# Outputs return on a list of their own; spatial weights and eight token blocks are turned by VectorE

## The chip, the core and the metric

The kernel runs on one core of one Trainium2 chip. TensorE (PE) multiplies, VectorE (DVE) and ScalarE (ACT) work element by element, GpSimd (POOL) and SyncE (SP) mostly issue DMAs, and 16 DMA engines move data between DRAM and the core's SBUF. [...] The metric is the device time of one execution in microseconds, the median of several runs; less is better.

## The reference, cut to what matters

One step of a decoder trunk with one layer, for a prompt of 256 tokens and 8 sample rows of one token, with a model width of 2048. A conditioning projection gives six vectors `sh, sc, gt` per row. Then:

```python
h = rmsnorm(x, g_pre_mix) * (1 + sc1) + sh1
z = h @ w_in                                   # splits into three branches and their gates
v = layernorm(gelu(z_v)); y_a = gelu(z_u) * (tril(w_s) @ v + b_s)      # 8 groups of 128x128
o, S = gated_linear_recurrence(q, k, v, log_f, s0)                     # y_b: HGRN2, 8 heads; y_c: GLA, 4 heads
merged = sum(sigmoid(z_gate[n]) * (y[n] @ w_branch[n]) for n in range(3))
x = x + gt1 * rmsnorm(merged @ w_out, g_post_mix)
h2 = rmsnorm(x, g_pre_mlp) * (1 + sc2) + sh2
x = x + gt2 * rmsnorm(square(relu(h2 @ w_mlp_up)) @ w_mlp_down, g_post_mlp)
```

Outputs are x for the prompt and the samples, the final recurrent states of both, and the normalised `v` rows of the samples. All is float32.

## The kernel before, in words

**Products.** Activations lie with channels on partitions and tokens (256 + 8 = 264, `NT`) along the free axis. A weight tile of 128x128 is the stationary operand and 264 tokens move. Each float32 product is made of three in a faster form: weights and activations are split into a high and a low part (`whi`, `wlo`), ScalarE makes the high part (L673), VectorE the low one (L677). `linear` makes a block of 256 output channels from granules of 1024 weight columns by 128 rows each; splits run two granules ahead (`SPLIT_AHEAD`), loads five (`LOAD_AHEAD`), weights come on SP's queue. A block accumulates in one of two PSUM buffers (`pmm`), which the next block but one needs back.

**Buffers.** 28 blocks of 128x1056 float32 (`NBLK`, `blk()`) hold activations and many temporaries.

**Stages.** First the conditioning and the first part of `w_in`, over k in five chunks (`CHUNKS`); in the last of these the loop counts `gi` from 0 to 19. Then the GLA inputs, branch 0 with spatial gating (`mixer_a`), the gates of branch b (`gate_tiles(5120)`), branch 1 (HGRN2, groups 0 and 1), the gates of branch c, branch 2 (GLA, group 2), the output projection (8 blocks `m`), the norms between, and the MLP in 8 slices with up and down projections; the last slice of the down projection ends the kernel.

**Order.** TensorE's and POOL's order is that of the program in the mixer stages; in the output projection and the MLP TensorE's alone is. VectorE and ScalarE are put in order by the compiler's scheduler in these stages, in order of program where it sees no wait. Each engine runs its own list strictly in order. Work of the mixers is written as generators on lists: `bg` (mixers, one after the other), `bs` (sample rows), `bt` (turns through DRAM). `background()` is called after each granule, one slot: it adds a rate to what a list may spend (`RATES` 1.8 to 1.0 for `bg`, 0.5 for `bs`, `TURN_RATE` 0.35 for `bt`) and steps the list's first generator; a step costs what it yields (1 for a bare `yield`). A generator that yields a function holds its whole list until it is true; `READY` holds it to the next slot. What is queued in `later` runs at the next slot. `finish(i)` drains the list up to group i's mixer before its outputs are used.

**Two ways to turn.** A 128x128 block is turned by TensorE against the identity into PSUM (L96; `to_tokens` does four of them for one block of two channel tiles by 256 tokens). Or through DRAM with the class `Rows`: `half` turns 32x32 squares with VectorE (L850), `out` writes 512 KB to `rows_d` (L853), `back` reads it in four DMAs of 128 KB that place the squares (L859); a copy then puts the rows in natural order. `TURN_OUT` and `TURN_IN` ask for two slots between these.

**What the change touches.** In `mixer_a` the spatial weights are turned by 8 TensorE transposes and masked with `triu` out of PSUM. In `mixer_r` the key block `kd` and the head outputs go through `Rows`; the mixer waits for both on its list (`kd_rows.come`, copies at L1462; `out.come`, `out.there`, copies at L1492), and only then does the list go on to the next mixer's `gates` (L1175 to L1179). Branch 1 begins with `parts_b`, that is `finish(0)`, `finish(1)` and the splits of `yparts` (L145, L148); its gate values leave PSUM by a `Tanh` at L1543. In the output projection each block is scaled (`gated`), turned by `to_tokens` one slot later, multiplied with the residual rows and squared for sums (`products` L1646, `squares` L1650), and copied to rows `og` (`put_rows` L1653, L1654). In the last slice of the down projection the same goes to `yt` without sums. `PRE_AT` names the blocks of the output projection at which two loads each (four blocks) of the sixth conditioning round are issued (L379).

Of the kernel before, what the change touches and what calls it, by code (L numbers as in the profile page):

```python
# [15 lines left out]
P = 128  # L16
# [30 lines left out]
N_PRE = 6  # L47
PRE_AT = (2, 3, 4)
ADA_BATCH = (4, 8)
# [23 lines left out]
def hybrid_step_kernel(  # L73
# [759 lines left out]

    rows_d = dp.tile([13, P, 1024], F32, tag="rows_d", name="rows_d")
    n_turned = [0]
# [69 lines left out]
    def const_a(src):  # L905
        consts_a.append(blk([P, 8, P]))
        nc.sync.dma_start(consts_a[-1], src)

    srcs_a = [
        sgu_ln_g[0].partition_broadcast(P).rearrange("p (g n) -> p g n", g=8),  # L910
        sgu_ln_b[0].partition_broadcast(P).rearrange("p (g n) -> p g n", g=8),
        sgu_w_s[0].rearrange("g n m -> n g m"),
        sgu_b_s[0].rearrange("g n -> (g n)").partition_broadcast(P).rearrange("p (g n) -> p g n", g=8),
# [34 lines left out]
    def mixer_a():  # L948
        lng, lnb, wsr, bsb = consts_a
        lng, lnb = (v.rearrange("p g n -> p (g n)") for v in (lng, lnb))  # L950
# [3 lines left out]
        for gg in range(2):  # L954
            ps = sm()
            for i in range(4):
                T.transpose(ps[:, i * P:(i + 1) * P], wsr[:, 4 * gg + i, :], ident)
            yield
            mul(wsT[:, 4 * gg:4 * gg + 4, :], ps.rearrange("p (g n) -> p g n", g=4), triu.unsqueeze(1).to_broadcast([P, 4, P]))
        yield  # L960
# [142 lines left out]
    for ci, n in enumerate(CHUNKS):  # L1103
# [5 lines left out]
        for gi in range(ng):  # L1109
# [35 lines left out]
            if final:  # L1145
                if gi in (6, 12, 18):
                    rounds.steps()
                if gi in (0, 2, 6, 8, 12, 14, 18):
                    rounds.load()
                if gi in (6, 7, 8, 9):  # L1150
                    rows_a.half((gi - 6) // 2, gi % 2)
                if gi in (8, 10):
                    rows_a.out(gi // 2 - 4)
                if gi in (11, 13):
                    rows_a.back((gi - 11) // 2)
                now[0] += 1
                if gi >= 12:
                    bg.pump(1.0)
# [163 lines left out]
    def mixer_r(G):  # L1322
# [98 lines left out]
        mul(kd, kd, k[:, :, 0:NP])  # L1421
        yield READY
        yield READY
        kd_rows = Rows([kd])
        yield from kd_rows.gone()
        attx = blk([P, 4, P])
        ps = sm([P, 4, P])
# [4 lines left out]
        del kd  # L1432
        yield from kd_rows.come()

# [7 lines left out]

        for hf in range(2):
            for h0 in range(0, 4, nh):
                ps = sm([P, nh, dv])
# [27 lines left out]
        for h0 in range(0, 4, nh):  # L1473
            so = blk([P, nh, dv])
            p0, p1 = sm([P, nh, dv]), sm([P, nh, dv])
            for i in range(nh):
                T.matmul(p0[:, i, :], kt[:, 0, (h0 + i) * P:(h0 + i + 1) * P], vr(0, h0 + i), start=True, stop=True)
                T.matmul(p1[:, i, :], kt[:, 1, (h0 + i) * P:(h0 + i + 1) * P], vr(1, h0 + i), start=True, stop=True)
            yield
            for i in range(nh):  # L1480
                S.activation(so[:, i, :], p0[:, i, :], AF.Copy, scale=ft[:, h0 + i:h0 + i + 1])
            add(so, so, p1)
            nc.gpsimd.dma_start(G.p_out(h0, nh), so)
            yield
        yield from out.come()
        yield out.there
        o = [blk() for _ in range(nj)]
        for a, rows in enumerate(out.rows):
            for hf in range(2):
                put = S.copy if hf else V.tensor_copy  # L1490
                for j in range(nj):
# [3 lines left out]
                    )  # L1495
                yield 0.6
        G.o = o

    def finish(i):
        bg.drain(gens[i])  # L1500
        G = Gs[i]
        while not hasattr(G, "os"):
            bs.drain(bs.g[0])
# [140 lines left out]
    def products(m, t, g, pt):  # L1644

        V.scalar_tensor_tensor(g[:, 1, 0:CW].rearrange("p (m f) -> p m f", m=2), in_rows(x1, t, m), 1.0, pt[:, t], ALU.mult, ALU.mult,  # L1646
                               accum_out=sums[:, 0, t, m:m + 1])

    def squares(m, t, g, pt):
        S.activation(g[:, 0, 0:CW].rearrange("p (m f) -> p m f", m=2), pt[:, t], AF.Square, accum_out=sums[:, 1, t, m:m + 1])  # L1650

# [4 lines left out]
    def block_rows(m, g):  # L1656
# [5 lines left out]
        for t in range(2):  # L1662
            squares(m, t, g, pt)

    def norms(meanwhile):
# [14 lines left out]

    sums = tmp([P, 2, 2, NS], "fs")
    pre = Rounds()
    pre.todo = [(5, k) for k in range(KT)]
    for m in range(8):
# [5 lines left out]
        if m < 7:  # L1690
            g = gated(m, z, G1)
            later.append((now[0], lambda m=m, g=g: block_rows(m, g)))
        if m == 6:

            S.activation(tmp([P, 1], "srr", 1), sqacc[:, 0:1], AF.Sqrt)
    rounds.drain()
    rounds = pre
# [36 lines left out]
    V.reduce_sum(both[:, :, 2:2 + NS], ps.rearrange("p s k b -> p s b k"), axis=mybir.AxisListType.X)  # L1734
    V.reduce_sum(both[:, :, 0:2], sums, axis=mybir.AxisListType.X)
    rounds.steps(3)
# [113 lines left out]
    def down(f, ah, al):  # L1850
        for m in range(8):
# [8 lines left out]
            if f == NFB - 1:  # L1860
                g = gated(m, dst, G2)
                later.append((now[0], lambda m=m, g=g: put_rows(m, to_tokens(g), yt)))

# [5 lines left out]
    for f in range(NFB):  # L1869
        nxt = up(f + 1) if f + 1 < NFB else None  # L1870
        if f == NFB - 1:
            rounds.drain()
            mul(G2, mod[:, 5 * KT:6 * KT, :], gpost2T.unsqueeze(2).to_broadcast([P, KT, NC]))
            yt = [[blk([P, 1024]) for _ in range(2)] for _ in range(2)]
        last = pend
        down(f, *pend)
# [151 lines left out]
```

## Time and profile before

| | |
|---|---|
| median of 3 runs | 1784.72 us (1784.36 to 1785.2) |
| profiled execution | 1786.63 us |
| its span, first to last instruction | 1784.6 us |
| mean granted TensorE clock | 0.998 |
| PEld, TensorE's weight loads, busy | 1676.9 us |
| DMA | 455.67 MB, mean 255 GB/s |

The page gives busy time by engine, then a row of 40 slices of the span. "Granted clock" is the share of full speed that TensorE had. The windows view gives, for a stretch in us from the start of the span: its length, the busy time of PE, PEld, DVE, ACT and POOL (with counts), the granted clock, the mean busy share of the DMA engines, and GB/s. The timeline gives start, length, engine, line, operation, and in brackets the engine's idle time before it and what ended that. In the lists of groups stand, after a bar, busy us, mean ns of one, and idle us before them with what ended it.

### The profile page before, as it was taken

The numbers are of one execution on the slowest core, as the hardware profiler recorded it, in microseconds if no ns is written. First come the engines' busy times: TensorE is split into PE (matmuls) and PEld (weight loads), VectorE is DVE, ScalarE is ACT, GpSimd is POOL, SyncE is SP. The second block draws the span as 40 slices with busy tenths as digits, with TensorE's granted clock in tenths as the row PEclk, the third lists the DMA queues.
The fourth block names the chain that finished last, engine by engine and source line by source line (L and its number), as shares of the span: only waits on it lengthen the run. The fifth ranks groups of instructions, "written<-read, shape, count | busy, mean of one in ns | idle before, by whom it ended". The sixth has DMA issues, their size and how long they took to land.

```text
span 1784.6 us, 42046 instructions
## 1 busy us (share of the span) xinstructions
PE 1760.2 (99%) x16866; PEld 1676.9 (94%) x16866; DVE 1194.0 (67%) x2096; ACT 999.7 (56%) x1810; POOL 175.6 (10%) x293
## 2 busy tenths in 40 slices
PE   6999999999999999999999999999999999999998
PEld 5899999999989989899999989999999999999997
DVE  5676669886687687666566666545666666666666
ACT  5444456667766665655555666545454545454554
POOL 4222010122111112220000010000000000000000
PEclk9999999999999999999999999999999999999999
DMA  9998699899999889998766847786666666666663
GB/s 345 395 354 297 224 327 306 253 331 325 301 290 311 284 276 333 347 374 281 222 193 217 310 124 238 234 263 197 193 198 193 198 194 196 195 196 196 195 195 115
DMA packets 334547, 455.67 MB, mean 255 GB/s; under 512 B 15986, under 2 KB 277984, under 8 KB 334352
## 3 DMA queue, kind: packets, MB, share of 16 engines
q1 hardware_dynamic: 312160, 381.05, 66.0%
q0 software_dynamic: 21552, 71.48, 11.6%
q8 instruction: 132, 2.16, 0.5%
q14 instruction: 63, 0.52, 0.1%
q10 hardware_dynamic: 640, 0.47, 0.1%
HBM read 434.42 MB, written 18.51 MB: 254 GB/s over the span
## 4 chain that ended last, share of the span: by engine, by line
PE 91%; DMA 4%; DVE 1%; issue 1%; ACT 1%; POOL 1%; SPq 0%; DVEq 0%; ACTq 0%; POOLq 0%
PE mm L92 83%; PE ada L92 4%; PE sm L92 3%; DMA raw<-in_w_in_dram 1%; DMA b<-in_w_ada_dram 1%; PE sm L96 1%; DVE wlo L677 0%; DMA b<-in_x_prompt_dram 0%; DMA out_dram<-st 0%; ACT whi L673 0%; DMA vbc<-vs_d 0%; POOL b L537 0%; DVE b L142 0%; DVE b L1768 0%; ACT b L148 0%
## 5 line engine op out<-in xcount | busy, mean ns | idle before, releaser
L92 PE MATMUL mm<-b,whi 128*128 128x264 f32 x9248 | 1580.1, 278 | 4.0 <-ACT gt L1543 2.9
L92 PEld LDWEIGHTS mm<-b,whi 128*128 128x128 f32 x9248 | 1397.2, 190 | 38.3 <-issue 19.8
L92 PE MATMUL mm<-b,wlo 128*128 128x264 f32 x4624 | 1278.8, 277 | 0.5 <-DVE wlo L677 0.5
L677 DVE TENSOR_TENSOR wlo<-raw,whi 128x512 fp32r<-128x512 f32 x1118 | 758.6, 689 | 421.9 <-ACT whi L673 419.1
L673 ACT CAST whi<-raw 128x512 fp32r<-128x512 f32 x1118 | 681.9, 617 | 635.0 <-DVE wlo L677 318.7
L92 PEld LDWEIGHTS mm<-b,wlo 128*128 128x128 f32 x4624 | 875.7, 189 | 1.1 <-DVE wlo L677 0.9
L142 DVE TENSOR_TENSOR b<-b,mm 128x528 f32<-128x528 f32 (+1 forms) x137 | 95.7, 699 | 71.7 <-PE mm L92 65.5
L1958 POOL TENSOR_TENSOR gs<-b,G 128x16 f32<-128x16 f32 x1 | 0.2, 222 | 713.9 <-DVE b L142 713.9
L92 PE MATMUL ada<-b,cT 128*32 128x256 f32 (+2 forms) x880 | 64.8, 419 | 2.8 <-DMA b<-in_w_ada_dram 2.8
L92 PEld LDWEIGHTS ada<-b,cT 128*32 128x32 f32 x880 | 25.9, 112 | 31.9 <-issue 16.2
L537 POOL DMA_DIRECT2D b<-in_w_ada_dram x64 | 46.3, 726 | 45.3 <-PE ada L92 36.0
L1307 POOL DMA_DIRECT2D out_dram<-st x32 | 23.5, 736 | 226.7 <-DVE st L1306 210.9
L673 ACT CAST whi<-araw 128x512 fp32r<-128x512 f32 x38 | 23.2, 618 | 28.4 <-PE mm L92 26.2
L92 PE MATMUL ada<-araw,cT 128*32 128x512 f32 x272 | 36.7, 599 | 0.0
L139 DVE TENSOR_TENSOR b<-b,b 128x512 f32<-128x512 f32 (+1 forms) x49 | 34.5, 721 | 2.2 <-ACT b L1367 0.7
L1304 ACT ACTIVATE st<-st,fs 128x128 f32<-128x128 f32 (+1 forms) x96 | 35.1, 427 | 0.0
L1306 DVE SCALAR_TENSOR_TENSOR st<-vbc,b,st 128x128 f32<-128x128 f32 (+1 forms) x96 | 32.2, 391 | 1.0 <-DMA vbc<-vs_d 1.0
L859 POOL DMA_DIRECT2D b<-rows_d x52 | 28.6, 556 | 31.1 <-DMA rows_d<-b 8.0
L677 DVE TENSOR_TENSOR wlo<-araw,whi 128x512 fp32r<-128x512 f32 x38 | 24.7, 686 | 1.7 <-ACT whi L673 1.6
L145 DVE TENSOR_TENSOR b<-b 128x1024 f32<-128x1024 f32 (+1 forms) x24 | 24.4, 1020 | 1.2 <-PE ada L92 1.1
L145 DVE TENSOR_TENSOR b<-gt,b 128x528 fp32r<-128x528 f32 x32 | 22.7, 711 | 3.2
L1842 ACT ACTIVATE b<-vt 128x528 fp32r<-128x528 f32 x32 | 22.8, 713 | 1.0
(307 smaller groups left out, 827.1 us busy)
## 6 DMA issues: line engine op xcount, KB each, us to landing
raw<-in_w_in_dram SPq DMA_DIRECT2D x225, 512.0 KB, 6.0
raw<-in_w_mlp_down_dram SPq DMA_DIRECT2D x128, 512.0 KB, 3.6
raw<-in_w_mlp_up_dram SPq DMA_DIRECT2D x125, 512.0 KB, 3.9
araw<-in_w_ada_dram SPq DMA_DIRECT2D x68, 512.0 KB, 6.8
b<-in_w_ada_dram SPq DMA_DIRECT2D x60, 512.0 KB, 6.7
b<-in_w_ada_dram POOLq DMA_DIRECT2D x48, 512.0 KB, 9.5
raw<-in_w_branch_dram SPq DMA_DIRECT2D x48, 512.0 KB, 4.9
raw<-in_w_out_dram SPq DMA_DIRECT2D x32, 512.0 KB, 4.6
```

The lines of the kernel that those rows point to most:

```text
L92: return nc.tensor.matmul(out, w, x, **kw)
L139: V.tensor_tensor(o, a, b, op=ALU.mult)
L142: V.tensor_tensor(o, a, b, op=ALU.add)
L145: V.tensor_tensor(o, a, b, op=ALU.subtract)
L537: queue.dma_start(w[:, i], w1[k * P:(k + 1) * P, :, self.k0 * P:(self.k0 + self.n) * P])
L673: self.last = [S.copy(hi, raw).ins, None]
L677: self.last[1] = V.tensor_tensor(lo, raw, hi.bitcast(F32), op=ALU.subtract).ins
L859: nc.gpsimd.dma_start(t[32 * q:32 * q + 32, :].rearrange("p (s c) -> p s c", s=4), rows_d[self.d0 + i].rearrange("(s p) (q c) -> q p s c", ...
L1304: S.activation(st[:, i, :], st[:, i, :], AF.Copy, scale=fs[:, h0 + i, b:b + 1])
L1306: V.scalar_tensor_tensor(st[:, i, :], v[:, i, :], k[:, h0 + i, NP + b:NP + b + 1], st[:, i, :], ALU.mult, ALU.add)
L1307: nc.gpsimd.dma_start(G.s_out(b, h0, nh), st)
L1842: S.activation(apart(a), by_two(rl), AF.Square)
```

## The change

Three things, and two that go with them. The spatial weights are turned by `Rows` during the last chunk (their constant is loaded first of the four), and the mask is multiplied from SBUF. Blocks 0 to 3 of the output projection and of the last down projection are turned in pairs by `Rows` (class `Pairs`); the sums of a pair are made over 512 columns once it is back. What a mixer does after its prompt states are written becomes the generator `outputs`, on the list `bt`; the return of `kd` is asked for only between the two halves of the outputs, and one `READY` ahead of its turn goes. The third batch of `PRE_AT` moves from block 4 to block 5, and `rows_d` grows from 13 to 19 tiles.

```diff
-PRE_AT = (2, 3, 4)
+PRE_AT = (2, 3, 5)
...
-    rows_d = dp.tile([13, P, 1024], F32, tag="rows_d", name="rows_d")
+    rows_d = dp.tile([19, P, 1024], F32, tag="rows_d", name="rows_d")
...
     def mixer_a():
...
         for gg in range(2):
-            ps = sm()
-            for i in range(4):
-                T.transpose(ps[:, i * P:(i + 1) * P], wsr[:, 4 * gg + i, :], ident)
+            mul(
+                wsT[:, 4 * gg:4 * gg + 4, :].rearrange("p k (s f) -> p k s f", s=4),
+                rows_w.rows[0][:, gg],
+                triu.rearrange("p (s f) -> p s f", s=4).unsqueeze(1).to_broadcast([P, 4, 4, 32]),
+            )
             yield
-            mul(wsT[:, 4 * gg:4 * gg + 4, :], ps.rearrange("p (g n) -> p g n", g=4), triu.unsqueeze(1).to_broadcast([P, 4, P]))
...
+                if gi == 0:
+                    rows_w = Rows(consts_a[0:1], lambda b, r: b[:, 4 * r:4 * r + 4, :].rearrange("p k (q f) -> p k q f", q=4))
+                if gi < 2:
+                    rows_w.half(0, gi)
+                if gi == 1:
+                    rows_w.out(0)
+                if gi == 4:
+                    rows_w.back(0)
...
         mul(kd, kd, k[:, :, 0:NP])
-        yield READY
-        yield READY
         kd_rows = Rows([kd])
         yield from kd_rows.gone()
+        yield READY
...
         del kd
-        yield from kd_rows.come()
...
         for hf in range(2):
+            if hf:
+                yield from kd_rows.come()
             for h0 in range(0, 4, nh):
...
             nc.gpsimd.dma_start(G.p_out(h0, nh), so)
             yield
+        G.tail = outputs(G, out)
+        bt.g.append(G.tail)
+
+    def outputs(G, out):
+        nj, nh = G.dv // P, 512 // G.dv
         yield from out.come()
         yield out.there
...
-                yield 0.6
+                yield 0.3
         G.o = o
...
         bg.drain(gens[i])
         G = Gs[i]
+        bt.drain(G.tail)
...
+    class Pairs:
...
+        def put(self, m, g):
+
+            i = m % 2
+            if i == 0:
+                self.r = Rows([None])
+                self.r.ts[0] = blk([P, 1024])
+            to = self.r.ts[0].rearrange("p (q r k f) -> p r k q f", q=4, r=2, k=4)
+            for t in range(2):
+                V.transpose(to[:, t, 2 * i:2 * i + 2], g[:, :, t * P:(t + 1) * P].rearrange("p k (q f) -> p k q f", q=4))
+            if i:
+                self.r.out(0)
+                self.soon(1, self.back, m // 2, self.r)
+
+        def soon(self, n, f, *a):
+            later.append((now[0] + n, lambda: f(*a)))
+            later.sort(key=lambda x: x[0])
+
+        def back(self, b, r):
+            r.back(0)
+            self.soon(2, self.natural, b, r.rows.pop())
+
+        def natural(self, b, v):
+
+            w = slice(b % 2 * 512, b % 2 * 512 + 512)
+            for t in range(2):
+                (V.tensor_copy if t else S.copy)(self.rows[t][b // 2][:, w].rearrange("p (k s f) -> p k s f", k=4, s=4), v[:, t])
+            self.then(b, w)
+
+    def block_sums(b, w):
+
+        for t in range(2):
+            junk = tmp([P, 512], "gt")
+            y = og[t][b // 2][:, w]
+            V.scalar_tensor_tensor(junk, x1[t][b // 2][:, w], 1.0, y, ALU.mult, ALU.mult, accum_out=sums[:, 0, t, b:b + 1])
+            S.activation(tmp([P, 512], "vt"), y, AF.Square, accum_out=sums[:, 1, t, b:b + 1])
...
+    pairs = Pairs(og, block_sums)
...
-            later.append((now[0], lambda m=m, g=g: block_rows(m, g)))
+            later.append((now[0], lambda m=m, g=g: block_rows(m, g) if m > 3 else pairs.put(m, g)))
...
-                later.append((now[0], lambda m=m, g=g: put_rows(m, to_tokens(g), yt)))
+                later.append((now[0], lambda m=m, g=g: put_rows(m, to_tokens(g), yt) if m > 3 else pairs.put(m, g)))
...
+            pairs = Pairs(yt, lambda b, w: None)
```

More of the change, by code (lines that the diff above doesn't have):

```diff
@@ L909, in hybrid_step_kernel @@
     srcs_a = [
+        sgu_w_s[0].rearrange("g n m -> n g m"),
         sgu_ln_g[0].partition_broadcast(P).rearrange("p (g n) -> p g n", g=8),
         sgu_ln_b[0].partition_broadcast(P).rearrange("p (g n) -> p g n", g=8),
-        sgu_w_s[0].rearrange("g n m -> n g m"),
         sgu_b_s[0].rearrange("g n -> (g n)").partition_broadcast(P).rearrange("p (g n) -> p g n", g=8),
@@ L948, in mixer_a @@
     def mixer_a():
-        lng, lnb, wsr, bsb = consts_a
+        _, lng, lnb, bsb = consts_a
         lng, lnb = (v.rearrange("p g n -> p (g n)") for v in (lng, lnb))
@@ L1646, in products @@
         V.scalar_tensor_tensor(g[:, 1, 0:CW].rearrange("p (m f) -> p m f", m=2), in_rows(x1, t, m), 1.0, pt[:, t], ALU.mult, ALU.mult,
-                               accum_out=sums[:, 0, t, m:m + 1])
+                               accum_out=sums[:, 0, t, m - 2:m - 1])
     def squares(m, t, g, pt):
-        S.activation(g[:, 0, 0:CW].rearrange("p (m f) -> p m f", m=2), pt[:, t], AF.Square, accum_out=sums[:, 1, t, m:m + 1])
+        S.activation(g[:, 0, 0:CW].rearrange("p (m f) -> p m f", m=2), pt[:, t], AF.Square, accum_out=sums[:, 1, t, m - 2:m - 1])
     def put_rows(m, pt, rows):
@@ L1663, in block_rows, with __init__ @@
             squares(m, t, g, pt)
+    class Pairs:
+        def __init__(self, rows, then):
+            self.rows, self.then = rows, then
+        def put(self, m, g):
[26 more added lines that the diff above has]
+            S.activation(tmp([P, 512], "vt"), y, AF.Square, accum_out=sums[:, 1, t, b:b + 1])
     def norms(meanwhile):
@@ L1691, in hybrid_step_kernel @@
             g = gated(m, z, G1)
-            later.append((now[0], lambda m=m, g=g: block_rows(m, g)))
+            later.append((now[0], lambda m=m, g=g: block_rows(m, g) if m > 3 else pairs.put(m, g)))
         if m == 6:
             S.activation(tmp([P, 1], "srr", 1), sqacc[:, 0:1], AF.Sqrt)
+    assert not later
     rounds.drain()
@@ L1734, in hybrid_step_kernel @@
     V.reduce_sum(both[:, :, 2:2 + NS], ps.rearrange("p s k b -> p s b k"), axis=mybir.AxisListType.X)
-    V.reduce_sum(both[:, :, 0:2], sums, axis=mybir.AxisListType.X)
+    V.reduce_sum(both[:, :, 0:2], sums[:, :, :, 0:6], axis=mybir.AxisListType.X)
     rounds.steps(3)
```

## The prediction

> **What bounds the kernel now.** I read the page first: the share of each engine, then the chain that ended last.
>
> ```profile
> PE 1760.2 (99%) x16866; PEld 1676.9 (94%) x16866; DVE 1194.0 (67%) x2096; ACT 999.7 (56%) x1810; POOL 175.6 (10%) x293
> ...
> PE 91%; DMA 4%; DVE 1%; issue 1%; ACT 1%; POOL 1%; SPq 0%; DVEq 0%; ACTq 0%; POOLq 0%
> ```
>
> TensorE carries 91% of the chain. So an instruction that leaves TensorE shortens the run by the time until the next one could start, and work added to another engine costs nothing until it makes TensorE wait. Two questions follow: what TensorE is spared, and which of its waits go or come. The chain in order of time, over the three places where the change takes transposes away, answers the first. Columns: start, length, what, count.
>
> ```profile
> 264.62 0.44 PE sm L96 x4
> ...
> 971.44 0.44 PE sm L96 x4
> 971.87 10.80 PE mm L92 x96
> 982.68 0.44 PE sm L96 x4
> ...
> 1733.45 0.44 PE sm L96 x4
> 1733.89 5.40 PE mm L92 x48
> 1739.29 0.44 PE sm L96 x4
> ```
>
> L96 is the helper of every TensorE transpose. Four of them take 0.44 us of the chain, and the period of a block is exactly matmuls plus that: 10.80 + 0.44 = 11.24 us in the output projection, 5.40 + 0.44 = 5.84 us in the last one. Nothing else stands between.
>
> For the second question, the groups of the page, the windows and the timeline around the only long stall in the middle of the run:
>
> ```profile
> L92 PE MATMUL mm<-b,whi 128*128 128x264 f32 x9248 | 1580.1, 278 | 4.0 <-ACT gt L1543 2.9
> ...
> 615.84 0.62 ACT L1492 COPY b<-b 128x512 f32<-128x512 f32 x1 [3.01 <-DMA b<-rows_d]
> 616.37 1.19 ACT L148 CAST b<-b 128x1056 fp32r<-128x1056 f32 x1
> ...
> 620.24 1.08 ACT L1175 ACTIVATE b<-b 128x1056 f32<-128x1056 f32 x1
> ...
> 623.34 1.28 ACT L1179 ACT_TABLE_LOAD   x1
> ...
> 627.03 0.61 ACT L1543 ACTIVATE gt<-mm 128x528 f32<-128x528 f32 x1
> ...
> 627.69 12.73 PE mm L92 x96
> ...
> 626.00:629.00 3.00, 1.31 (x7) 1.31 (x8) 2.93 (x5) 2.99 (x5) 0.00 (x0) 0.86 0.89 306
> 629.00:632.00 3.00, 3.00 (x17) 3.00 (x17) 3.00 (x6) 1.45 (x4) 0.00 (x0) 0.57 0.38 99
> ```
>
> At the start of the second branch ScalarE idles 3.01 us for the returned outputs of recurrent group 1 (L1492). Then it has at once the splits of `yparts` (L148), the gates of the GLA group that come next on the list (L1175 to L1179, with a table load) and the `Tanh` (L1543) that frees a PSUM buffer. TensorE waits 2.9 us for that `Tanh`. Behind it 96 matmuls take 12.73 us where 10.80 is the rule: 1.93 us more, because the granted clock fell to 0.57 in the window from 629. The place costs 2.9 + 1.9 = 4.8 us. The Trainium skill ("TensorE: Matmul & The Clock Gate", Part 1) says that an idle window of about 3.4 us halves TensorE's clock; the trace agrees in kind, with 2.9 us of idling ahead of the halved clock.
>
> **The change, part by part.**
>
> *Transposes leave TensorE.* Spatial weights: 2 sets of four. Blocks 0 to 3 of the output projection: 4 sets. The same blocks of the last projection: 4 sets. 10 sets x 0.44 us = 4.40 us, all on the chain. Whether the longer records of these transposes count instead is the first rival.
>
> *What takes their place on VectorE, ScalarE and the DMA queues.*
>
> ```profile
> L850 DVE STREAM_TRANSPOSE b<-b x26: 666/705/712, 243.1 to 740.0; 128x512 f32<-128x512 f32 x26
> ...
> L1646 DVE SCALAR_TENSOR_TENSOR gt<-b,sm 128x256 f32<-128x256 f32 x14 | 5.9, 418 | 1.2 <-PE sm L96 0.5
> L1654 DVE COPY b<-sm 128x256 f32<-128x256 f32 x7 | 2.9, 418 | 0.0
> L677 DVE TENSOR_TENSOR wlo<-raw,whi 128x512 fp32r<-128x512 f32 x61 | 42.1, 692 | 25.3 <-ACT whi L673 25.1
> ...
> 724.01 0.43 DVE L1462 COPY b<-b 128x512 f32<-128x512 f32 x1 [4.49 <-DMA b<-rows_d]
> ...
> 971.87:983.11 11.24, 11.24 (x103) 11.24 (x102) 7.64 (x17) 6.90 (x16) 0.00 (x0) 1.00 0.84 292
> 983.11:994.35 11.24, 11.24 (x103) 11.24 (x102) 7.64 (x17) 6.85 (x16) 0.00 (x0) 1.00 1.03 368
> ...
> 1733.89:1739.73 5.84, 5.84 (x54) 5.84 (x54) 4.73 (x10) 3.68 (x8) 0.00 (x0) 1.00 0.61 184
> ```
>
> The spatial weights need two 128x512 transposes, 2 x 0.70 us, in a stage in which TensorE never waits; the masking multiply stays. A pair of blocks needs four transposes of 128x256. None is in the trace: at most the 0.70 us of one twice as large, at least half, 0.35; I take 0.38, near half, as these instructions grow with their columns. In the output projection a pair then loses four products and two copies of 0.42 us (2.5 us) and gains 1.5 us of transposes, a copy of 0.43 us (L1462's) and two products over 512 columns (0.7 us each, the length of a 512-column operation at L677): 15.3 - 2.5 + 3.4 = 16.2 us of VectorE in two periods of 10.80 us. Room enough. In the last projection there were no products: 9.5 - 0.8 + 1.5 + 0.4 = 10.6 us in 10.8 us. VectorE is nearly full for four blocks; with 0.70 us a transpose it would need 11.9 us and fall 1.1 us behind per pair, 2.2 us in all. Splits run two granules (5.4 us) ahead, so I count 0.5 us for this place, bounds 0 and 2.2. ScalarE's side gets smaller.
>
> *The round trip and its waits.* Each pair writes 512 KB to DRAM and reads it back in four DMAs issued by POOL, which is idle there. The copies out of the returned block sit in VectorE's and ScalarE's order; if the data are late, all that is queued behind them waits, weight splits and evictions of PSUM included, and TensorE behind those. The same construction is in the trace; the first row is that of the reads back, the others the chain while VectorE waited at 724:
>
> ```profile
> DMA to landing us min/median/max: 4.2/7.1/9.5
> ...
> 719.12 2.70 PE mm L92 x24
> ...
> 723.55 2.70 PE mm L92 x24
> ```
>
> The longest such wait of VectorE, 4.49 us ahead of 724.01, passed with TensorE going on: look-ahead covered it. In the last projection the DMA engines are at 0.61, so I expect landings near the 4.2 us end; in the output projection they are at 1.03 and it will be the other end, but VectorE has room there. I count nothing beyond the 0.5 us above; with the cover gone each of four returns could cost TensorE up to 4.5 us.
>
> *`PRE_AT` 3rd batch one block later.* Two loads of w_ada, four blocks. It gives the pairs buffers: 24 of 28 blocks are taken by x1, og, the split operands and two batches. The batch is first used after block 7, over 20 us later, so it lands in time. But it sits in SP's order ahead of weight loads, and if the second pair's buffers are not free, these wait behind it. In this stage ScalarE never waited for a load (the row names TensorE, VectorE and itself alone):
>
> ```profile
> L673 ACT CAST whi<-raw 128x512 fp32r<-128x512 f32 x60 | 37.0, 617 | 31.7 <-PE mm L92 30.7 <-DVE wlo L677 0.7 <-ACT whi L673 0.3
> ```
>
> I take nothing, bounds 0 and 4 us. The order of the four constants changes no count.
>
> *Outputs on a list of their own.* No instruction is removed; the list of mixers no longer stands still while `kd` and the outputs travel.
>
> ```profile
> 447.52 0.56 POOL L853 DMA_DIRECT2D rows_d<-b  x1 [9.80 <-DVE b L850]
> 455.05 0.77 POOL L1483 DMA_DIRECT2D out_dram<-b  x1 [6.97 <-DVE b L142]
> ...
> 467.77 0.61 ACT L1492 COPY b<-b 128x512 f32<-128x512 f32 x1
> 468.27 1.08 ACT L1175 ACTIVATE b<-b 128x1056 f32<-128x1056 f32 x1
> ...
> 598.52 0.56 POOL L853 DMA_DIRECT2D rows_d<-b  x1 [19.78 <-DVE b L850]
> 605.28 0.76 POOL L1483 DMA_DIRECT2D out_dram<-b  x1 [6.20 <-DVE b L142]
> 607.12 2.20 POOL L859 DMA_DIRECT2D b<-rows_d  x4 [1.09 <-PE ada L92]
> ...
> L96 PE MATMUL sm<-cst,os x4: 273/273/331, 605.9 to 825.6; 128*128 128x128 f32 x4
> ```
>
> Group 0's prompt states left at 455.05, but group 1's gates began at 468.27, right behind group 0's outputs (467.77): 13 us of standing still. Group 1's states left at 605.28; 13 us sooner, and by my estimate two slots (5 us) more for each of the two `kd` returns, is about 582, with the rows out at 575.5 in place of 598.52. From 598.52 to the copies at 615.84 is 17 us, so 593; its own list, at 0.35 a slot, can add three slots of 2.7 us: 601, against the 606 at which `finish` needs them (first L96 of `os`). So the outputs are there, the splits of `yparts` come while the first 10.8 us of matmuls run, and the GLA gates move from 620 to some 582, into a stage whose evictions are 10.8 us apart. I take the whole 4.8 us as gained, the upper bound too; the lower is 0. The margin of 5 us is worked out from rows of another pace; it is the weakest step.
>
> **Sum.** -4.40 - 4.8 + 0.5 = -8.7 us. The profiled execution took 1786.63 us (span 1784.6 and 2.0 around it) and would take 1777.9; against the median of the runs, 1784.72, it gives **1776.0 us**.
>
> **Rivals.**
>
> *Each transpose is worth its whole record* (2%).
>
> ```profile
> L96 PE MATMUL sm<-cst,gt x84: 272/273/329, 25.3 to 1773.8; 128*128 128x128 f32 x84
> ```
>
> 40 x 0.273 us = 10.9 us in place of 4.40 gives 1769.5. Against it: starts lie 0.11 us apart (0.44 per four). The Trainium skill ("TensorE: Matmul & The Clock Gate", Part 4) gives about 275 ns for one in a kernel's context, and the record agrees with that, but the chain does not charge it. The same skill ("VectorE: DVE Perf Modes", Rules for kernel authors) would leave 128x128 transposes on TensorE where PSUM suits; by that the change is a loss, and the chain speaks against it as long as VectorE has room.
>
> *The stall stays, or its like appears elsewhere* (20%): the outputs are again late at `finish`, or the moved gates delay another `Tanh`. Only 4.40 - 0.5 is gained: 1780.8. For it: the margin of 5 us. Against: 13 us at group 0 alone.
>
> *The returns are late where TensorE waits for the same engines* (16%): blocks 4 to 6 keep their TensorE transposes, which wait for `gated` on VectorE and ScalarE. One or two returns stand ahead of it and cost 2 to 4 us each: 1778 to 1783. For it: the 10.6 us of 10.8.
>
> *Slower* (7%): all four returns hold VectorE beyond its look-ahead. Once a wait outlasts the 4.5 us that were covered by over 2.9 us, TensorE idles as it did at 625 and the slow clock adds 1.9 us. 4 x 4.8 us = 19 us against the 8.7 us gained: 1795. It decides from 12.3 us lost, 3.1 us a return. For it: 9.5 us landings. Against: VectorE's room in the output projection and quiet DMA in the last.
>
> **How the numbers follow.** Forecast 55%, at 1776.0; its own bounds are 1774.4 (no loss in the last projection, and the other 1.1 us of idling in the first TensorE row gone too) and 1777.7 (2.2 us lost there); the rivals 2, 20, 16 and 7%. To hold eight in ten the range takes in the stall that stays and most of the late returns: 1774.4 to 1782.3. A change under 0.2% (3.6 us) can't be told from none, so faster means under 1781.2 and slower over 1788.3. Faster: 55 + 2 + 12 of the 20 + 10 of the 16 = 79%; the rest of these two, 14%, is no change; slower 7%.
>
> **What would show it.** Right: periods of 10.80 and 5.40 us between blocks in the chain; 40 fewer L96 transposes; no PE wait on L1543 and a clock of 1.00 in all windows between 600 and 650; L1175 of the last group some 30 us earlier. Wrong: VectorE or ScalarE waiting over 4.5 us for rows_d after 980 with TensorE idle behind it, a stall in the last 50 us, SP held at L379 with weight loads behind it, or a granted clock under 1 anywhere past 60 us.

## The result: 0.4% slower, with the expected gain in the chain

The changed kernel took 1792.24 us (median of 13 runs, 1786.80 to 1796.86) against 1786.01 us (13 runs) for the kernel before on the same chip: a ratio of 1.0040, interval 1.0030 to 1.0049. Ratios, here and below, are estimated with 95% intervals from the fast executions alone (e3, e4 and e13 each have one more of over 4700 us), so they are not exactly the quotient of the two medians, 1.0035 here. The forecast was 1776.0 us, the range 1774.4 to 1782.3. The profiled execution took 1791.95 us, with a span of 1790.2 us and a mean granted clock of 0.996.

Two things came as forecast. First two lines of the page of the changed kernel, its busy times and its chain, then one row of the chain in order of time (start, length, what, count):

```profile
PE 1761.7 (98%) x16826; PEld 1676.2 (94%) x16826; DVE 1194.4 (67%) x2100; ACT 996.5 (56%) x1798; POOL 189.5 (11%) x318
...
PE 93%; DMA 3%; DVE 1%; ACT 1%; issue 1%; SPq 0%; POOL 0%; ACTq 0%; DVEq 0%
```

```profile
959.91 53.23 PE mm L92 x473
```

40 instructions fewer on TensorE (16866 before). Where the chain before had 0.44 us of transposes after each 10.80 us, it now runs 53.23 us of matmuls without a break. Then the start of branch 1, first the windows (start:end, length, busy time of PE, PEld, DVE, ACT and POOL, clock, DMA share, GB/s), then the timeline of ScalarE:

```profile
626.00:629.00 3.00, 3.00 (x72) 2.96 (x59) 3.00 (x7) 0.84 (x2) 0.71 (x1) 1.00 0.95 285
629.00:632.00 3.00, 3.00 (x30) 2.46 (x30) 2.24 (x5) 2.89 (x6) 1.26 (x2) 1.00 1.00 355
```

```profile
578.95 1.10 ACT L1184 ACTIVATE b<-b 128x1056 f32<-128x1056 f32 x1
...
592.24 0.62 ACT L1506 COPY b<-b 128x512 f32<-128x512 f32 x1
```

PE was busy 1.31 us of the first window before and the clock was 0.57 in the second; now both are full. The last group's gates (L1175 before, L1184 now) began at 578.95 rather than 620.24, and the outputs of the group ahead of it, group 1, were copied at 592.24 (615.84 before).

What was not forecast stands at two places. At 750 TensorE waits for conditioning weights (`w_ada`). The chain, the waits of TensorE from 735 to 770 (in all, times, longest), and the windows there:

```profile
741.28 13.29 DMA b<-in_w_ada_dram
...
754.61 1.92 PE ada L92 x4
```

```profile
PE ada L92 <- DMA b<-in_w_ada_dram: 2.8, 2, 2.2
```

```profile
753.00:757.00 4.00, 3.40 (x10) 0.82 (x11) 2.18 (x5) 0.47 (x1) 0.72 (x1) 0.62 1.06 393
757.00:760.00 3.00, 3.00 (x16) 3.00 (x15) 0.06 (x1) 0.62 (x1) 0.01 (x1) 0.50 1.06 406
```

That is 2.8 us of waiting and some 3 us of slow clock.

And at 1022 to 1038, where the second pair of the output projection returns. The timeline, all engines:

```profile
1007.69 0.56 POOL L853 DMA_DIRECT2D rows_d<-b  x1 [16.96 <-DVE b L1693]
...
1013.25 0.56 POOL L859 DMA_DIRECT2D b<-rows_d  x1 [4.99 <-PE mm L92]
...
1022.96 0.62 ACT L1710 COPY b<-b 128x512 f32<-128x512 f32 x1 [7.61 <-DMA b<-rows_d]
1022.98 0.43 DVE L1710 COPY b<-b 128x512 f32<-128x512 f32 x1 [6.76 <-DMA b<-rows_d]
...
1024.15 0.49 PE L92 MATMUL mm<-b,whi 128*128 128x264 f32 x2 [1.14 <-ACT whi L673]
...
1031.13 0.47 ACT L1646 ACTIVATE gt<-mm,G 128x256 f32<-128x256 f32 x1 [0.22 <-DVE gt L1643]
...
1031.65 1.11 PE L96 MATMUL sm<-cst,gt 128*128 128x128 f32 x4 [3.63 <-ACT gt L1646]
```

```profile
1029.00:1032.00 3.00, 0.35 (x2) 0.35 (x3) 2.60 (x6) 2.78 (x6) 0.00 (x0) 0.74 0.71 213
1032.00:1035.00 3.00, 3.00 (x16) 3.00 (x15) 1.83 (x8) 0.10 (x1) 0.00 (x0) 0.50 0.64 196
1035.00:1038.00 3.00, 3.00 (x18) 3.00 (x18) 1.03 (x2) 1.24 (x3) 0.00 (x0) 0.62 0.59 182
```

The chain behind the wait (start, length, what, count):

```profile
1031.65 1.11 PE sm L96 x4
1032.77 13.06 PE mm L92 x96
```

How to read it: from POOL's write to the copies, the pair travels 15 us. ScalarE and VectorE come to the copies (L1710) 7.6 and 6.8 us before the data are there, and all that stands behind waits too: first the splits (TensorE loses 1.14 us for `whi`), then, in a burst, the copies, the pair's sums, the products and squares of block 4, and last `gated` of block 5 (L1646), for which block 5's transposes stand still 3.63 us. The clock in the three windows from 1029 is 0.74, 0.50 and 0.62. The transposes behind the wait take 1.11 us where 0.44 is the rule, and the 96 matmuls 13.06 us where 10.80 is: 2.9 us lost to the slow clock. The place costs 1.14 + 3.63 + 2.9 and 0.3 us for a low part (`wlo`), some 8 us. The first pair's copy waited too, 4.75 us at 998, and TensorE waited for nothing from 975 to 1010.

### The profile page after: what moved, and what is told of

Read it like the earlier page. It is cut to its first block, busy times and chain, and to the rows that moved or that the text cites. A ratio compares the mean times of both kernels' runs of the same rounds, so it can differ in the third digit from the quotient of the medians.

```text
span 1790.2 us, 42033 instructions
## 1 busy us (share of the span) xinstructions
PE 1761.7 (98%) x16826; PEld 1676.2 (94%) x16826; DVE 1194.4 (67%) x2100; ACT 996.5 (56%) x1798; POOL 189.5 (11%) x318
## 4 chain that ended last, share of the span: by engine, by line
PE 93%; DMA 3%; DVE 1%; ACT 1%; issue 1%; SPq 0%; POOL 0%; ACTq 0%; DVEq 0%
PE mm L92 85%; PE ada L92 5%; PE sm L92 3%; DMA raw<-in_w_in_dram 2%; DMA b<-in_w_ada_dram 1%; DVE wlo L677 1%; PE sm L96 0%; DMA b<-in_x_prompt_dram 0%; DMA b<-rows_d 0%; DVE b L142 0%; DVE b L1826 0%; ACT whi L673 0%; SPq L537 0%; ACT b L148 0%; DVE b L145 0%
## 5 line engine op out<-in xcount | busy, mean ns | idle before, releaser
L142 DVE TENSOR_TENSOR b<-b,mm 128x528 f32<-128x528 f32 (+1 forms) x137 | 95.4, 697 | 68.8 <-PE mm L92 62.7
L853 POOL DMA_DIRECT2D rows_d<-b x18 | 10.1, 563 | 927.1 <-DVE b L1693 852.0
L859 POOL DMA_DIRECT2D b<-rows_d x72 | 39.6, 556 | 57.1 <-DMA rows_d<-b 15.5
```

The costliest lines, as they stand in the source:

```text
L142: V.tensor_tensor(o, a, b, op=ALU.add)
L859: nc.gpsimd.dma_start(t[32 * q:32 * q + 32, :].rearrange("p (s c) -> p s c", s=4), rows_d[self.d0 + i].rearrange("(s p) (q c) -> q p s c", ...
```

## The experiments

Every ratio below is against the kernel before, run on the same chip.

| | what is in it | median, us | ratio (interval) |
|---|---|---|---|
| changed | all | 1792.24 | 1.0040 (1.0030 to 1.0049) |
| e1 | list of outputs alone | 1781.02 | 0.9969 (0.9957 to 0.9980) |
| e2 | all but the list | 1797.45 | 1.0064 (1.0050 to 1.0078) |
| e3 | all, third batch at block 6 | 1791.06 | 1.0025 (1.0015 to 1.0035) |
| e4 | e3, copies held back | 1791.60 | 1.0027 (1.0017 to 1.0038) |
| e5 | all, planner's count kept | 1791.02 | 1.0034 (1.0021 to 1.0047) |
| e6 | list, last projection | 1779.84 | 0.9966 (0.9954 to 0.9978) |
| e7 | e6, spatial weights, count kept | 1782.37 | 0.9982 (0.9973 to 0.9992) |
| e8 | e5, only blocks 0, 1 of the output projection | 1787.84 | 1.0013 (1.0000 to 1.0026) |
| e9 | e6, output projection, third batch at block 5 | 1790.04 | 1.0017 (1.0007 to 1.0026) |
| e10 | list, spatial weights, count kept | 1783.21 | 0.9984 (0.9976 to 0.9993) |
| e11 | e9, next block in its slot | 1785.43 | 0.9996 (0.9986 to 1.0006) |
| e12 | e11, copies late and spread | 1785.67 | 0.9999 (0.9989 to 1.0008) |
| e13 | e11, loads of w_ada apart | 1783.82 | 0.9991 (0.9982 to 1.0000) |
| e14 | e12, loads of w_ada apart | 1778.97 | 0.9966 (0.9955 to 0.9978) |

**e1 and e2, the two halves.** e1 is the kernel before with the part of the diff on `mixer_r`, `outputs` and `finish`; e2 is the changed kernel without that part:

```diff
+        G.tail = outputs(G, out)
+        bt.g.append(G.tail)
+
+    def outputs(G, out):
...
+        bt.drain(G.tail)
```

> The kernel before with the outputs on their own list and the later return of kd alone; all transposes stay on TensorE, PRE_AT stays (2, 3, 4). Theory: the stall at the start of branch 1 goes (5.3 us with the slow clock behind it) and a stall of 4 to 5 us with 3.4 us of slow clock comes near 750, where TensorE waits for w_ada: about 2 us slower than before, ratio 1.001 (0.999 to 1.003). Rival, that the wait near 750 belongs to the blocks turned by VectorE or to that one execution: no such wait, 5 us faster, ratio 0.997.

> The changed kernel with the mixers' list as before: spatial weights, pairs of blocks and PRE_AT as changed. Theory: 10 sets of transposes leave TensorE (-4.4 us), the stall at the start of branch 1 stays, and the second pair of the output projection costs some 9.5 us (6 us of stall, 3.4 us of slow clock): 5 us slower than before, ratio 1.003, with ScalarE waiting over 6 us for rows_d near 1020. Rival, that the late return needs the other list's timing: 4 us faster, ratio 0.998, no wait over 5 us.

e1 gave 1781.02 us, 5.1 us under the 1786.14 of the kernel before beside it. The stall at branch 1 is gone (windows), and no wait for `w_ada` came at 750, so the list did not bring that one:

```profile
626.00:629.00 3.00, 3.00 (x28) 2.46 (x22) 2.84 (x7) 1.81 (x3) 0.30 (x1) 1.00 1.05 375
629.00:632.00 3.00, 3.00 (x29) 3.00 (x28) 3.00 (x6) 2.46 (x5) 0.06 (x1) 1.00 0.97 279
```

It brought a smaller wait, which the kernel before does not have (waits of TensorE, 540 to 560):

```profile
PE sm L92 <- DVE b L139: 1.8, 1, 1.8
```

e2 is slower than the changed kernel, so the list gains beside the turns too, and the turns lose more than the list brings. TensorE's waits for `w_ada` (1.44 us at 768, 2.06 us at 771) are in e2: the turns bring them. One thing in e2's trace speaks against its theory: the stall at branch 1 is missing there too (clock 1.00 from 600 to 650, TensorE idle for 1.2 us), though the last group's gates still begin at 617. The profiled execution was the fastest of the five, 1793.75 us against 1796.49 to 1798.17, so the others may have it; the traces do not show by what the list gains beside the turns.

**e3 and e4, the output projection.** e3 moves the third batch of `PRE_AT` from block 5 to block 6; e4 also runs the copies two slots later and behind the newest weight split:

```diff
-PRE_AT = (2, 3, 5)
+PRE_AT = (2, 3, 6)
...
-            self.soon(2, self.natural, b, r.rows.pop())
+            self.soon(4, self.natural, b, r.rows.pop())
...
+            with tc.issue_after(stream[0].last[0]), tc.issue_after(stream[0].last[1]):
```

> The changed kernel with the third batch of w_ada loads at block 6 in place of 5. Theory of place (the copies of the second pair stand in ScalarE's and VectorE's order ahead of their data, by the round trip's usual 15 us): the wait stays over 6 us, time within 0.15% of the changed kernel, ratio to before 1.003 to 1.004. Rival, contention with the third batch: the wait falls under 4.5 us, the stall and the slow clock go, 9 us less than the changed kernel, ratio 0.999.

> The changed kernel with the copies of a returned pair held behind the latest weight split, four slots after the read (two in the last projection) and the third batch at block 6. Theory of place: ScalarE and VectorE wait under 1 us for rows_d in the output projection, TensorE has no stall and a full clock from 1000 to 1045, about 9.5 us less than the changed kernel, ratio to before 0.999. Rival, that the stall comes of the DMA load and the weights arriving late: it stays, ratio 1.003 to 1.004.

e3 came out just under its theory and e4 missed. In e3 TensorE's wait for `gt` stayed 3.6 us, while ScalarE's wait for the data fell from 7.6 to 6.0 us: the third batch made a part of it, which by the medians is worth nothing beside the early copies (e13 and e14 take the two apart). In e4 (timeline) the copies waited for 1.76 us at most, and TensorE still did, for `gated` of block 5:

```profile
1023.91 0.62 ACT L1711 COPY b<-b 128x512 f32<-128x512 f32 x1 [1.76 <-DMA b<-rows_d]
...
1028.98 0.66 PE L96 MATMUL sm<-cst,gt 128*128 128x128 f32 x4 [2.38 <-ACT gt L1646]
```

TensorE's order shows why: the transposes of block 4 stand in the wrong place. `soon` sorts `later`, but a block's own entry is appended behind the pair's, and the list is worked off from the front. So the block behind a returned pair is turned 24 matmuls late in the changed kernel and 72 late in e4, and its products and squares fall in with the pair's. In e4 that and the held copies can't be told apart.

**e5, the wait at 750.** The planner counts TensorE's instructions (`T.n`); with 8 transposes gone from `mixer_a` (two counts each), what it slots in later, conditioning steps among them, stands elsewhere in the order. e5 is the changed kernel with `T.n += 8` ahead of each `yield` behind the masked product.

> The changed kernel with the planner's count of TensorE instructions raised by 8 at each of the two places in mixer_a where four transposes stood, so that small products of the mixers fall into the slots in which they fall with the list alone. Theory (the count shifts by 16, the plan of slots shifts with it, and a step of the w_ada rounds is taken before its weights have landed): no wait of TensorE over 1 us between 60 and 1000, full clock there; the second pair's stall near 1022 stays; ratio to before 0.9995 (0.998 to 1.001). Rival, that the wait near 750 comes of the spatial weights' round trip itself (buffers, DMA): it stays, ratio 1.003.

The wait for `w_ada` is gone; from 735 to 770 TensorE's waits are now:

```profile
PE mm L92 <- ACT gt L1559: 1.5, 2, 1.0
```

So the place of the step in TensorE's order made that wait, and neither the list nor the round trip of the spatial weights. By the ratios it is worth 1.0034 against 1.0040, which the intervals do not separate and which misses the forecast of 0.9995: other waits came in its place, of 1.2 us for `w_ada` at 278 and of 2.7 us at 549 with a slow clock behind it (0.58 from 554 to 558). The wait at 549 is that of e1; the shifted order of the changed kernel had been without it.

**e6, e7 and e10, the parts at the two ends.** e6 is the changed kernel with the spatial weights and the output projection on TensorE as before; e7 adds the spatial turn to e6 and e10 adds it to e1, both with the count kept.

> The outputs on their own list and blocks 0 to 3 of the last projection turned by VectorE; spatial weights and the output projection by TensorE as before, PRE_AT (2, 3, 4). Theory: the list's gain and 4 sets of 0.44 us more, waits for rows_d after 1700 under 2.5 us, no TensorE stall from them: ratio 0.996 (list alone measured 0.9969). Rival, that VectorE is too full there: 2 us lost in the last 50 us, ratio 0.997 to 0.998.

> As the changed kernel, but the output projection's transposes all on TensorE with PRE_AT (2, 3, 4), and the planner's count kept as before (8 more at two places). Theory: list 5.5 us, last projection 1.8 us, spatial weights 0.9 us: ratio 0.9954, no TensorE wait over 1 us between 60 and 1700 but the norms after the output projection. Rival, that the spatial round trip delays VectorE near 265 by as much as it saves: ratio 0.996 or above.

> The list and the spatial weights' turn by VectorE with the plan's count kept; both projections turn on TensorE as before. Against the kernel with the list alone (1781.02 us, 0.9969) only the two sets of four transposes (0.88 us) leave TensorE. Theory: the round trip's 512 KB out and four reads of 128 KB stand beside the weight loads between 230 and 285, and TensorE waits there for loads of w_ada and weights 1 to 2 us in all: 1782 to 1783 us, ratio 0.997 to 0.9985. Rival: the two sets are worth their 0.88 us: 1780.1, ratio 0.9964; no wait of TensorE over 0.5 us between 230 and 285 that the kernel with the list alone does not have.

The last projection does no harm: a copy waits 2.15 us and TensorE goes on. In the traces of e1 and e6 its four sets of transposes are gained in full (1.75 us, by the starts of the matmuls); the medians can't show it, for the 0.0003 against e1 are within the intervals. The spatial turn should save 0.88 us and costs 0.0015 to 0.0016 of the time, 2.7 to 2.9 us. Windows 235 to 245 of e1 and of e10, then from each the row of DMA issues from 235 to 285 (the last number is the median us to landing):

```profile
235.00:245.00 10.00, 10.00 (x89) 8.44 (x88) 6.35 (x10) 5.45 (x9) 0.00 (x0) 1.00 0.81 286
```

```profile
235.00:245.00 10.00, 10.00 (x83) 7.90 (x83) 6.22 (x10) 4.58 (x9) 2.20 (x4) 1.00 1.03 344
```

```profile
raw<-in_w_in_dram SPq DMA_DIRECT2D x16, 512.0 KB, 7.4
```

```profile
raw<-in_w_in_dram SPq DMA_DIRECT2D x16, 512.0 KB, 9.4
```

Of the windows from 235 to 285 this alone had room in the DMA engines (0.81; the others stand at 0.98 to 1.06). The round trip fills it, weights land 2 us later, and TensorE, which had no wait from 235 to 285 in e1, gets 0.9 us for VectorE (L142) and 0.2 us for `w_ada`, and its weight loads 2.3 us for `w_ada`. By the starts of the matmuls e10 loses 2.4 us against e1 between 43 and 298. That the full DMA engines are the cause is read from these rows; no run moves the round trip to another place.

**e8 and e9, the output projection by itself.** e8 is e5 with blocks 2 and 3 back on TensorE; e9 is e6 with the pairs of the output projection.

> As the changed kernel with the planner's count kept, but only the first pair (blocks 0 and 1) of the output projection turned by VectorE; blocks 2 to 7 by TensorE; PRE_AT (2, 3, 5). Theory of place and look-ahead: ScalarE and VectorE wait 4 to 5.5 us for rows_d near 998 and TensorE does not stop, since what it needs next is already split; ratio 0.995. Rival, that any such wait stops TensorE here, or that the third batch at block 5 does it: a stall of over 2 us between 995 and 1035 and a slow clock, ratio 0.998 or above.

> The list, both projections' pairs, spatial weights on TensorE as before: against the kernel with the list and the last projection's pairs (1779.84 us, 0.9966) only the four turned blocks of the output projection are added, and the plan's count of instructions is that of before. Theory: these four blocks save 1.76 us of transposes and cost 8 to 9 us in waits and slow clock, so about 1787 us, ratio 0.999 to 1.002; no wait of TensorE for w_ada of over 1 us near 750, but VectorE and ScalarE wait 5 us and more for rows_d between 995 and 1030, and TensorE stands still for at least 3 us in all behind the copies of one of the two pairs, followed by a granted clock of 0.5. Rival: the loss in the output projection needs the spatial round trip and its DMA load ahead of it; then the four blocks are worth their 1.76 us and the time is 1778, ratio 0.996.

e9 minus e6 is 0.0051 of the time: 9.1 us lost where 1.76 us were to be saved (e9 also has the third batch at block 5, where e6 has it at block 4). e8 minus e7, one pair and the same move of the batch, is 0.0031, 5.5 us. e5 and e8 show that the wait for the data is not by itself the price. The first pair's copy and the longest wait of TensorE behind it, in e5, where the next two blocks are not turned by TensorE, then in e8, where they are:

```profile
998.46 0.62 ACT L1711 COPY b<-b 128x512 f32<-128x512 f32 x1 [5.91 <-DMA b<-rows_d]
...
1000.50 0.38 PE L92 MATMUL mm<-b,wlo 128*128 128x264 f32 x1 [0.23 <-DVE wlo L677]
```

```profile
1005.70 0.62 ACT L1711 COPY b<-b 128x512 f32<-128x512 f32 x1 [5.71 <-DMA b<-rows_d]
...
1014.40 0.90 PE L96 MATMUL sm<-cst,gt 128*128 128x128 f32 x3 [3.64 <-ACT gt L1647]
```

The same wait costs 0.23 us in one and 3.64 us and a slow clock in the other. The splits that run ahead cover it; what has no cover is `gated` of the next block that TensorE turns. (In e8 block 2 is also turned 24 matmuls late; e11 takes that apart. The profiled execution of e8 was its slowest, 10 us over its median, with waits of 2.6 us at 549 and 5.6 us between 735 and 800 besides, so its total says nothing.)

**e11 to e14, the causes apart.** e11 mends the order of `later` in e9; e12 also holds the copies back as e4 does and makes a pair's sums one per slot (the sums were not tried by themselves); e13 and e14 are e11 and e12 with the two loads (four DMAs) of each batch of `PRE_AT` two slots apart:

```diff
 later.append((now[0], lambda m=m, g=g: block_rows(m, g) if m > 3 else pairs.put(m, g)))
+            later.sort(key=lambda x: x[0])
...
-            for _ in range(n):
-                pre.load(True)
+            pre.load(True)
+            later.append((now[0] + 2, lambda: pre.load(True)))
+            later.sort(key=lambda x: x[0])
```

> The kernel of e9_list_pairs with one line more: the helper list is sorted again when a block is entered in it, so that the block behind a returned pair is turned by TensorE in its usual slot and not one slot (24 matmuls, 2.7 us) later, behind the pair's copies. The copies themselves keep their place in ScalarE's and VectorE's order, right behind the eviction of block 4. Theory: what decides is that the copies stand there some 7 to 8 us before their data land; the waits of 7.96 and 7.11 us stay, TensorE still waits over 3 us for the evictions of the block behind, and the time is that of e9: 1788 to 1791 us, ratio 1.0005 to 1.002. Rival: the late turn of block 4, whose products, copies and squares then fall between the pair's copies and the next eviction, is what stops TensorE; with it in its slot the wait falls under 1 us and no slow clock follows: 1781 to 1783 us, ratio 0.997 to 0.9985.

> The kernel of e11_pairs_sorted with the copies of the output projection's pairs held four slots behind the read in place of two, and behind the weight splits issued by then, so that they stand six splits (some 8 us) later in ScalarE's and VectorE's order, and with the sums of a pair one per slot behind them. Theory: the copies then meet data that have landed; waits for rows_d under 2 us each, no wait of TensorE over 1 us between 990 and 1035 and a clock of 1.00 there; the four blocks are worth their 1.76 us: 1777 to 1779 us, ratio 0.9945 to 0.9965, under both kernels and at or under e6_list_last (0.9966). Rival: the added copies, products and squares are by themselves too much for the two engines beside the blocks that TensorE turns; TensorE loses 3 us or more there again, and the ratio is 0.998 or higher.

> The kernel of e11_pairs_sorted with the two loads of w_ada of each batch of PRE_AT two slots apart in place of together, so that a weight load stands behind one of them and not behind both, at the blocks where the pairs return. The copies keep their early place. Theory (two causes, each enough alone): the reads back and the weight loads land sooner, some 9 us in place of 12 to 14 for the latest weight load between 985 and 1020, but the copies still stand ahead of their data; waits for rows_d fall from 7.9 to 5 or 6 us and TensorE still waits over 1.5 us for an eviction behind the second pair: 1783 to 1785.5 us, ratio 0.9985 to 0.9995 (e11: 0.9996). Rival: the burst of loads alone makes the loss; waits for rows_d under 4 us, no wait of TensorE over 1 us between 990 and 1035: 1777.5 to 1780 us, ratio 0.9955 to 0.9965.

> The kernel of e12_pairs_spread with the same loads two slots apart: copies late and no burst. Theory (two causes): with both removed neither the copies nor the weight splits wait over 2 us between 990 and 1035, TensorE has no wait over 1 us and a clock of 1.00 there, and the four blocks are worth their 1.76 us: 1777 to 1780 us, ratio 0.995 to 0.9965, under e12 (0.9999) by 3 thousandths or more. Rival: the queue carries too much there in whatever order (512 KB out and in per pair beside weights and w_ada); a weight load between 1000 and 1020 still takes over 11 us, TensorE waits over 2 us and the ratio is 0.998 or higher.

e11 fell between its two theories: 0.0021 better than e9 (3.8 us), with the copies waiting as long. In e12 no copy waits, and TensorE stands still all the same, since ScalarE now waits for a late weight load ahead of `gated` (timeline; then the landing times of the weights issued from 1003 to 1015, min, median, max):

```profile
1019.00 1.14 ACT L673 CAST whi<-raw 128x512 fp32r<-128x512 f32 x2 [6.31 <-DMA raw<-in_w_out_dram]
...
1020.05 0.61 ACT L1702 COPY b<-b 128x512 f32<-128x512 f32 x1
...
1022.25 1.06 PE L96 MATMUL sm<-cst,gt 128*128 128x128 f32 x4 [4.75 <-ACT gt L1637]
```

```profile
DMA to landing us min/median/max: 8.2/10.8/13.7
```

The chain of e12 has that weight load:

```profile
1005.17 13.73 DMA raw<-in_w_out_dram
```

Four DMAs of `w_ada`, 2 MB, go out on SP between 1001 and 1005 and the pair's reads at 1005.5. The last three of the four and the weight load behind them (issued at 1005.17) land one after the other at 1013.9, 1016.5, 1017.7 and 1018.9, the weights 13.7 us after their issue; weights issued in the same stretch take at most 6.7 us in the kernel before. e13 takes the burst away and leaves the copies early (waits of the engines, 990 to 1035):

```profile
ACT b L1701 <- DMA b<-rows_d: 12.5, 2, 7.3
```

```profile
PE sm L96 <- ACT gt L1637: 2.4, 2, 2.2
```

e14 takes both away. Its chain, the one wait of ScalarE for a weight from 990 to 1035, and the landing times:

```profile
954.97 57.60 PE mm L92 x512
```

```profile
ACT whi L673 <- DMA raw<-in_w_out_dram: 1.2, 1, 1.2
```

```profile
DMA to landing us min/median/max: 4.0/7.3/8.9
```

TensorE waits for nothing from 990 to 1035. So there are two causes, and either is enough: with the early copies or with the burst the ratio is 0.9991 to 0.9999, with neither it is 0.9966.

The traces say the same of this stage alone. By the starts of the same matmuls, the stretch from 958 to 1042 us of the kernel before takes longer by 7.1 us in the changed kernel, 8.6 in e9, 7.3 in e11, 4.9 in e12 and 3.2 in e13, and is 1.6 us shorter in e14: 4 x 0.44 = 1.76 as forecast, less 0.17 us at the transposes of block 5. So the order of `later` is worth 1.3 us in these traces, against 3.8 us by the ratios of e9 and e11. The median does not show e14's gain: e14 and e6 have the same ratio, and both lie under the kernel before and the changed one. Nor can totals of single traces show it. Between 539 and 838 us, where e6, e9 and e11 to e14 are the same program, they gain 1.5 to 6.9 us on the kernel before: least where the slow clock followed the wait at 549 (e9, e14), most where that wait was short (0.6 us in e12, 1.5 us in e13).

**The sum.** In thousandths of the time: list -3.1 (e1), last projection -0.3 (e6 less e1), output projection +5.1 (e9 less e6), spatial weights +1.6 (e7 less e6). Together they give +3.3, against +3.4 of e5, which has these four. The planner's count, the changed kernel less e5, is +0.6. Each of these carries an interval of one thousandth or more to each side, so that the sum agrees to 0.1 is luck.

## Why the prediction was wrong, step by step

- *Transposes leave TensorE, 4.40 us*: right as a mechanism. The periods are 10.80 and 5.40 us, and e14 shows the gain where nothing takes it back. The rival that counts whole records is out.
- *List of outputs, 4.8 us, "the weakest step"*: right in kind. The stall and its slow clock are gone, the gates came at 579 (forecast some 582), the outputs at 592 (601). That the medians of e1 give 5.1 us is partly luck: the like of the stall that a rival feared did come, at 549 (1.8 us in e1), what made up for that wait is not known, and e2's trace is without the stall though it has no such list.
- *Turning on VectorE*: 0.38 us each was the estimate; two together took 0.77 us. *Last projection, 0.5 us of loss*: no loss in the trace of e6; VectorE was not too full.
- *"The round trip and its waits ... I count nothing"*: the step that failed most. The output projection lost 5.1 thousandths, 9.1 us, where 1.76 us were to be gained. The waits came at the far end of the price and beyond: 7.6 us against 4.5. The cover was read off a place in the trace (4.49 us of VectorE at 724, where ScalarE waited 2.66 us) at which TensorE had no `gated` to wait for. In the output projection it needs `gated` in time for the next transposes. The third rival named this ("blocks 4 to 6 keep their TensorE transposes, which wait for `gated`") and took 2 to 4 us a return; one return cost some 8 us with the slow clock. The reads themselves landed within the 9.5 us that were taken (4.6 to 7.9 us); but ScalarE stood before its copy at 1015.35, 2.1 us after the first of them was issued. That a burst of loads would make the weights late was not weighed.
- *`PRE_AT`, "I take nothing, bounds 0 and 4 us"*: wrong, and for another reason than the one weighed. SP was not held up (0.4 us at L379); the batch's four DMAs went out together, from 1009.66 to 1013.05, with the pair's return, and weights and reads came late: weights up to 12.7 us after their issue from 1003 to 1015 (6.7 before), reads up to 7.8 us (6.5 in e3, where the batch is a block later); a block earlier was not run with the pairs. As the causes are each enough alone, this one has no price of its own.
- *"Spatial weights ... in a stage in which TensorE never waits"*: wrong. That TensorE had no wait was taken for room, but the DMA engines stand at 0.98 to 1.06 there but for one window of 10 us (e1's windows, and those of the kernel before alike); the turn costs 2.7 to 2.9 us rather than gaining 0.88.
- Not seen at all: the entry order of `later` (3.8 us by the ratios of e9 and e11, 1.3 us in their traces), readable from the diff; and that fewer transposes move what a planner slots in by count (the wait at 750).
- *Slower* was given 7%, by four returns of 4.8 us each. In the changed kernel's trace it came from one return and from the wait at 750: the return's wait of 7.6 us is 3.1 us beyond the 4.49 us that were covered, and the slow clock followed, but mostly through `gated` and not through the splits (3.63 us against 1.14).

## What to carry to other kernels

Before work is moved from a full engine to a round trip through DRAM, read the DMA share and the landing times of the very windows in which it will travel, and ask of each engine that will wait for it what stands behind the wait and which consumer has the least slack; look-ahead that covers one consumer says nothing of another. Put the consumers of returned data behind the work that must not wait, and don't let a prefetch batch start beside the return. Where order is worked out by counts or lists, compare the order of all engines before and after, for a removed instruction moves others.

## What the runs showed of the hardware

- A wait of TensorE of 2 us or more can cost about as much again by a slow clock, or nothing more. One of 3.63 us (changed kernel) was followed by 6.8 us at 0.50, one of 2.20 us (e11) by 3.4 us, one of 2.2 us (e13) by none, and at 549 waits of 2.5 us (e9) and 2.8 us (e14) by 3.4 us, of 2.9 us (e11) and 3.0 us (e6) by none. The Trainium skill ("TensorE: Matmul & The Clock Gate", Part 1) has a free-running window of 3.413 us, and the stretches here are one or two of them. So waits shorter than that were enough; what decides between such waits, no run here shows.
- A load lands later behind others on its queue: 4.4 us (median, 1003 to 1015) for the weights of the output projection before, 13.7 us behind four `w_ada` DMAs in e12, 8.9 us at most in e14, where these lie apart. The Trainium skill ("DMA: Bandwidth & Descriptors", Queues, rings and completion order) says that each engine takes its descriptors in ring order, and these rows agree.
- Two STREAM_TRANSPOSEs of 128x256 float32 take 0.77 us back to back, 0.38 us each, though the record of one is 0.44 us long (median of 16 in the changed kernel). One of 128x512 has a record of 0.70 us.
